# A two-layer trunk on one core: the FFN up-projections as 2x2 block products in seven multiplications

## The chip, the cores and the metric

The kernel runs on 1 core of one Trainium2 chip, in one launch. The metric is the device time in microseconds. Five engines matter: PE (TensorE, matmuls; PEld are its weight loads), DVE (VectorE), ACT (ScalarE), POOL (GpSimd) and SP (SyncE, which issues most DMAs). Tiles lie in SBUF; matmuls write to PSUM, which POOL doesn't read here.

## The reference, cut to what matters

Layer 0 is a retention block, layer 1 a differential attention; behind each stands the same kind of FFN, on 1024 positions of 1024 values, with D_FF = 2816. Only the FFN's up-projection changes:

```
def conv_ffn(xn, w_up, conv_w, conv_b, w_down):
    S = xn.shape[1]
    h = xn @ w_up                       # (1024 x 1024) @ (1024 x 5632)
    hp = jnp.pad(h, ((0, 0), (CONV_WIDTH - 1, 0), (0, 0)))
    hc = conv_b
    for j in range(CONV_WIDTH):         # causal, width 3, per channel
        hc = hc + hp[:, j:j + S] * conv_w[j]
    g, u = jnp.split(hc, 2, axis=-1)
    return (jax.nn.silu(g) * u) @ w_down

    x = x + rms_norm(h, a_norm_post[i])                  # end of the block before
    h = conv_ffn(rms_norm(x, ffn_norm_pre[layer]), ...)
    x = x + rms_norm(h, ffn_norm_post[layer])
```

## The kernel before

Every float32 operand of a matmul is kept as a high and a low part (`split_to`, L81: ACT rounds to the high part, DVE subtracts to get the low one), and a product is three matmuls: high x high, high x low, low x high (`mm3`, L96). Weights come through `load_w` (L85): a DMA on SP's queue into one of the two buffers of `raw`, POOL multiplies in the norm's gain where there is one, and ACT and DVE split into one of five `hl` buffers. PSUM has four tiles of 128 x 1024.

An FFN runs in `gated` (L479) over 22 blocks of 128 channels, in groups of 1, then nine times 2, then 3. For each block f, `up(f)` (L617) computes two column blocks of the up-projection, the gate's and the other (`proj_t`, 2 x 48 matmuls of 512 columns), the convolution out of PSUM (`conv`, L596: one ACT and two DVE instructions per column block), then silu on ACT, the product on POOL and the split of the result into one of three `act` buffers. `down` (L501) then multiplies a group's blocks by their rows of w_down for the 8 blocks of 128 positions, 12 matmuls each for a group of two, and DVE adds each PSUM result to `acc`. The down products of one group stand between the up-projections of the next. The last block is done in two halves (`up_last`, L652), whose second half stands between the first products of the last group.

`finish` (L129) is the end of a block: per 128 positions the norm, the residual, and for the next stage the transposes into `xt` (`into_xt`, L123); its last steps stand between the first up-projections. A scheduler places the instructions of every engine by their readiness and keeps program order only inside the stretches marked as manual; a buffer of a pool is reused when the last reader of its old tile is done, and DMAs stand in SP's queue in the order in which the scheduler put them. A wait at the head of an engine's queue holds everything behind it.

## Time and profile before

| | us |
|---|---|
| median of 3 runs | 2941.19 (2940.98 to 2942.84) |
| the profiled execution | 2942.96, its span 2941.2 |
| busy: PE, PEld | 2880.3, 2436.4 |
| busy: DVE, ACT, POOL | 1469.9, 946.5, 668.4 |
| granted TensorE clock, mean | 0.995 of full speed |

A share of busy time is a mean over stages: the first FFN lies between about 865 and 1608 us of the span, the second between about 2175 and the end. What a change inside a stage is worth is read from that stage's rows: how many matmuls, at which distance, and what ended the idle time before them. A granted clock of 1.00 is 2.4 GHz, 0.50 is 1.2 GHz.

### The profile page before, as it was taken

What the parts mean: (1) busy time and instruction counts of PE and PEld (TensorE: products, weight loads), DVE (VectorE), ACT (ScalarE), POOL (GpSimd) and SP (SyncE); (2) the same over time, 40 slices, a digit from 0 to 9 for tenths busy, and PEclk for the clock granted to TensorE, in tenths of its full rate; (3) what the DMA queues carried; (4) which work ended last, traced back from release to release, by engine and by line L of the source; (5) the groups of instructions that cost most, each with busy time, mean ns of one, the idle gap of its engine ahead of it and who ended that gap; (6) DMA issues with size and microseconds to landing.
All of it is one profiled execution on the core that took longest, in us unless ns stands there. A gap on an engine that the chain in (4) does not pass through costs nothing. (4 is left out here: it accounts for less than half of the span.)

```text
span 2941.2 us, 35261 instructions
## 1 busy us (share of the span) xinstructions
PE 2880.3 (98%) x14452; PEld 2436.4 (83%) x14452; DVE 1469.9 (50%) x1722; ACT 946.5 (32%) x1462; POOL 668.4 (23%) x744
## 2 busy tenths in 40 slices
PE   8999999999999999999999999999999999999998
PEld 7898989888877888888888788888777888888886
DVE  4433433434446444444445687777554444444445
ACT  3323222211134222222224565555453222222222
POOL 1111120000033111211114334444332121121113
PEclk9999999999999999999999999999999999999999
DMA  4111111321232111111113332233252111111112
GB/s 141 53 54 51 51 52 37 121 79 59 78 122 86 51 50 43 51 50 51 43 44 120 118 80 75 68 85 93 73 204 80 43 50 51 47 47 44 58 58 100
DMA packets 86225, 210.45 MB, mean 72 GB/s; under 512 B 9648, under 2 KB 35248, under 8 KB 86064
## 3 DMA queue, kind: packets, MB, share of 16 engines
q1 hardware_dynamic: 62432, 180.67, 19.3%
q10 hardware_dynamic: 23632, 27.53, 2.9%
q8 instruction: 114, 1.87, 0.3%
q14 instruction: 47, 0.39, 0.0%
HBM read 164.12 MB, written 31.46 MB: 66 GB/s over the span
## 5 line engine op out<-in xcount | busy, mean ns | idle before, releaser
L97 PE MATMUL ps<-xh,hl 128*128 128x512 f32 x1952 | 764.3, 392 | 3.7 <-DVE xl L83 2.4
L99 PE MATMUL ps<-xh,hl 128*128 128x512 f32 x1952 | 762.3, 391 | 0.0
L98 PE MATMUL ps<-xl,hl 128*128 128x512 f32 x1952 | 760.0, 389 | 0.5 <-DVE xl L83 0.5
L492 PE MATMUL ps<-hl,act 128*128 128x512 f32 x2880 | 664.5, 391 | 1.1 <-DVE acc L508 1.1
L492 PEld LDWEIGHTS ps<-hl,act 128*128 128x128 f32 x2880 | 540.8, 188 | 114.3 <-DVE acc L508 1.9
L604 DVE SCALAR_TENSOR_TENSOR hc<-ps,cw,hc 128x1023 f32<-128x1023 f32 (+4 forms) x184 | 226.6, 1232 | 536.8 <-ACT hc L600 536.5
L90 POOL TENSOR_TENSOR raw<-raw,gains 128x1024 f32<-128x1024 f32 x120 | 238.0, 1984 | 1124.3 <-DMA raw<-in_w_up 1032.7
L99 PEld LDWEIGHTS ps<-xh,hl 128*128 128x128 f32 x1952 | 366.9, 188 | 79.7
L97 PEld LDWEIGHTS ps<-xh,hl 128*128 128x128 f32 x1952 | 367.0, 188 | 79.6 <-DVE xl L83 2.6
L98 PEld LDWEIGHTS ps<-xl,hl 128*128 128x128 f32 x1952 | 366.8, 188 | 78.8 <-DVE xl L83 1.0
L82 ACT ACTIVATE hl<-raw 128x1024 fp32r<-128x1024 f32 x228 | 240.0, 1054 | 500.3 <-PE ps L492 320.0
L83 DVE TENSOR_TENSOR hl<-raw,hl 128x1024 fp32r<-128x1024 f32 x228 | 289.9, 1272 | 114.2 <-ACT hl L82 114.0
L510 DVE TENSOR_TENSOR acc<-ps,acc 128x1024 f32<-128x1024 f32 x192 | 234.6, 1222 | 148.4 <-PE ps L492 147.1
L600 ACT ACTIVATE hc<-ps,cw 128x1024 f32<-128x1024 f32 (+1 forms) x92 | 107.6, 1170 | 485.1 <-PE ps L99 475.7
L611 POOL TENSOR_TENSOR hc<-hc 128x1024 f32<-128x1024 f32 x42 | 100.8, 2400 | 346.8 <-DVE hc L604 319.9
L97 PE MATMUL ps<-hl,xh 128*128 128x256 f32 x544 | 154.9, 286 | 1.7 <-ACT xh L82 1.7
L99 PE MATMUL ps<-hl,xl 128*128 128x256 f32 x544 | 155.3, 286 | 0.8 <-DVE xl L83 0.7
L98 PE MATMUL ps<-hl,xh 128*128 128x256 f32 x544 | 154.8, 285 | 0.0
L853 ACT ACTIVATE s<-s,m 128x256 f32<-128x256 f32 (+7 forms) x128 | 99.1, 775 | 102.1 <-POOL m L852 101.7
L82 ACT ACTIVATE act<-hc 128x1024 fp32r<-128x1024 f32 (+1 forms) x46 | 47.1, 1024 | 239.9 <-POOL hc L611 231.1
L97 PEld LDWEIGHTS ps<-hl,xh 128*128 128x128 f32 x544 | 105.2, 194 | 2.8 <-ACT xh L82 2.6
L99 PEld LDWEIGHTS ps<-hl,xl 128*128 128x128 f32 x544 | 105.3, 194 | 1.6 <-DVE xl L83 1.5
(188 smaller groups left out, 3701.1 us busy)
## 6 DMA issues: line engine op xcount, KB each, us to landing
raw<-in_w_up SPq DMA_DIRECT2D x88, 512.0 KB, 3.5
raw<-in_w_down SPq DMA_DIRECT2D x44, 512.0 KB, 3.5
raw<-in_w_t SPq DMA_DIRECT2D x32, 512.0 KB, 3.5
xold<-x SPq DMA_DIRECT2D x24, 512.0 KB, 4.6
raw<-in_w_v SPq DMA_DIRECT2D x16, 512.0 KB, 3.5
oret<-t ACTq DMA_DIRECT2D x32, 256.0 KB, 2.3
raw<-in_a_w_out SPq DMA_DIRECT2D x16, 512.0 KB, 3.6
on<-oret SPq DMA_DIRECT2D x16, 512.0 KB, 4.6
```

The lines of the kernel that those rows point to most:

```text
L82: nc.scalar.activation(out=hi, in_=src, func=AF.Copy)
L83: nc.vector.tensor_tensor(out=lo, in0=src, in1=hi.bitcast(F32), op=ALU.subtract)
L90: nc.gpsimd.tensor_tensor(out=v, in0=v, in1=gain.unsqueeze(2).broadcast_to([P, gain.shape[1], n]), op=ALU.mult)
L97: nc.tensor.matmul(out, sh, mh, start=start, stop=False)
L98: nc.tensor.matmul(out, sh, ml, start=False, stop=False)
L99: nc.tensor.matmul(out, sl, mh, start=False, stop=stop)
L492: nc.tensor.matmul(ps[:, half, :], a, ws[f][:, m, hs], start=f == 0 and n == 0, stop=f == len(ws) - 1 and n == 2)
L510: nc.vector.tensor_tensor(out=acc[sb], in0=flat(ps), in1=acc[sb], op=ALU.add)
L600: nc.scalar.activation(out=hc[:, c0:c1], in_=ps[:, c0:c1], func=AF.Identity, scale=cw[0][:, n, 2:3], bias=cw[0][:, n, 3:4])
L604: nc.vector.scalar_tensor_tensor(out=hc[:, b:c1], in0=ps[:, b - j:c1 - j], scalar=cw[0][:, n, 2 - j:3 - j], in1=hc[:, b:c1], op0=ALU.mult, ...
L611: eng.tensor_tensor(out=hg[:, cs], in0=hg[:, cs], in1=hu[:, cs], op=ALU.mult)
L853: nc.scalar.activation(out=s[:, :w], in_=s[:, :w], func=AF.Exp, scale=0.125, bias=m, accum_out=l[:, c:c + 1])
```

## The change

The up-projection of a block f, [gate; other] = [A11 A12; A21 A22] x [X11 X12; X21 X22], is taken as a 2x2 block product: the rows are the two column blocks of w_up, the inner halves are k = 0 to 3 and 4 to 7, the columns are the two halves of 512 positions. Seven products of 4 x 3 matmuls (`prod`) take the place of eight, in Winograd's form: sums of A (s1 = A21 + A22, s2 = s1 - A11, A11 - A21, A12 - s2) are made by POOL in `weights(f)` and split into a ring of eight `wc` buffers; sums of X (t1, t2, t3, t4 and X22) are made once per layer by DVE and POOL and split. DVE adds the products' results while it takes them out of PSUM (`plus`), ACT copies out the first two. The products A11 X11 and A12 X21 of the first four f stand in the tail of the stage before and behind it. The norm's gain is now multiplied into the rows before the transposes (DVE, `finish`), no longer into the weights by POOL; `Staged` keeps the transposed rows of X unsplit as well.

The convolution reads SBUF tiles, not PSUM. Each finished block is stored to DRAM on ACT's queue, and only when all 22 are done a second phase runs `gated`, in which `up` is `stored`: load a block back through `raw`, split it into an `act` buffer. `up_last` is gone. Matmuls on a PSUM bank that already holds a product are added onto it (`onto`). In the second layer's output projection `load_o` takes its rows through `raw` too.

```diff
...
             nc.tensor.transpose(ps[:, k, :], xn[:, k * P:(k + 1) * P], ident)
         return ps
+    class Staged:
+        def __init__(self, pool, gain):
+            self.gain = gain
+            self.h, self.l = (pool.tile([P, NK, 512], F32R, name=f"x{n}0", tag=f"x{n}0") for n in "hl")
+            self.raw = [pool.tile([P, NK, 512], F32, name=f"xraw{c}", tag=("xh1", "xl1")[c]) for c in range(2)]
+            self.pool = pool
+        def put(self, ps, c, cols):
+            if c == 0:
+                split_to(self.h[:, :, cols], self.l[:, :, cols], ps)
+            nc.scalar.activation(out=self.raw[c][:, :, cols], in_=ps, func=AF.Copy)
     def into_xt(ps, sb, xt):
-        xh, xl = xt
         c, b = divmod(sb, 4)
         cols = slice(b * P, (b + 1) * P)
+        if isinstance(xt, Staged):
+            xt.put(ps, c, cols)
+            return
+        xh, xl = xt
         split_to(xh[c][:, :, cols], xl[c][:, :, cols], ps)
     def finish(mm, add, pool, psp, gpost, x_old, x_new, xt, order=tuple(range(NS)), turn_first=False, late=()):
...
                     xh = live["xh", c] = pool.tile([P, D], F32, name="xhn", tag="w4")
-                    nc.scalar.activation(out=xh, in_=live.pop(("t", c)), func=AF.Copy, scale=live.pop(("q", c)))
+                    if isinstance(xt, Staged):
+                        nc.vector.scalar_tensor_tensor(out=xh, in0=live.pop(("t", c)), scalar=live.pop(("q", c)),
+                                                       in1=xt.gain, op0=ALU.mult, op1=ALU.mult)
+                    else:
+                        nc.scalar.activation(out=xh, in_=live.pop(("t", c)), func=AF.Copy, scale=live.pop(("q", c)))
...
         return up
-    def ffn_up(wk, layer, xt, tail, w_pool=None, late=None, on_drained=None):
-        cw = []
-        gpre = gains4[:, 2 + layer, :]
...
+    def ffn_up(layer, xt, tail, w_pool, late, on_drained):
+        N_PRE = 4
+        acts = [dram.tile([P, S], F32, name=f"act{layer}_{f}") for f in range(NF)]
+        K0, K1 = slice(0, 4), slice(4, 8)
+        X11, X21 = ((xt.h[:, ks], xt.l[:, ks]) for ks in (K0, K1))
+        def prod(out, w, x, onto=False):
+            for k in range(4):
+                ws = slice(k * P, (k + 1) * P)
+                mm3(out, w[0][:, ws], w[1][:, ws], x[0][:, k, :], x[1][:, k, :], not onto and k == 0, k == 3, onto)
+        def load_halves(f, half):
+            raw = rawp.tile([P, 1024], F32, name="raw")
+            for u in range(2):
+                nc.sync.dma_start(out=raw[:, COLS[u]], in_=A["w_up"][layer, f + u][:, COLS[half]])
+            return raw
+        w_first = {}
+        def load_pre():
+            for f in range(0, N_PRE, 2):
+                hl = w_pool.tile([P, 2, 1024], F32R, name="hl", tag="hl")
+                split_to(hl[:, 0, :], hl[:, 1, :], load_halves(f, 0))
+                for u in range(2):
+                    w_first[f + u] = hl[:, 0, COLS[u]], hl[:, 1, COLS[u]]
+        if late is None:
+            load_pre()
+        else:
+            late.append(load_pre)
+        pre = []
+        for f in range(N_PRE):
+            if f % 2 == 0:
+                next(tail)
+                pre.append(psp.tile([P, 2, 512], F32, name="ps"))
+            prod(pre[-1][:, f % 2, :], w_first[f], X11)
+        for _ in tail:
+            pass
+        st = ExitStack()
+        on_drained()
+        up = st.enter_context(tc.tile_pool(name=f"u{layer}", bufs=7, reuse_waits="tile"))
+        sp = st.enter_context(tc.tile_pool(name=f"s{layer}", bufs=3, reuse_waits="tile"))
+        cp = st.enter_context(tc.tile_pool(name=f"c{layer}", bufs=1, reuse_waits="tile"))
+        ring = st.enter_context(tc.tile_pool(name=f"ring{layer}", bufs=8, reuse_waits="tile"))
+        gp = st.enter_context(tc.tile_pool(name=f"gu{layer}", bufs=1, reuse_waits="tile"))
+        cw = gp.tile([P, 2 * NF, 4], F32, name="cw")
+        nc.sync.dma_start(out=cw, in_=A["conv"][layer])
+        def half_tile():
+            return up.tile([P, 512], F32, name="u")
+        first = {}
+        def copied(f, bank):
+            first[f] = half_tile()
+            nc.scalar.activation(out=first[f], in_=bank, func=AF.Copy)
+        def split_part(src, eng=nc.vector):
+            t = ring.tile([P, 2, 512], F32R, name="wc")
+            nc.scalar.activation(out=t[:, 0, :], in_=src, func=AF.Copy)
+            eng.tensor_tensor(out=t[:, 1, :], in0=src, in1=t[:, 0, :].bitcast(F32), op=ALU.subtract)
+            return t[:, 0, :], t[:, 1, :]
+        for f in range(N_PRE):
+            if f % 2 == 0:
+                raw = load_halves(f, 1)
+            w = split_part(raw[:, COLS[f % 2]])
+            bank = pre[f // 2][:, f % 2, :]
+            copied(f, bank)
+            prod(bank, w, X21, True)
+        names = ("t2", "t3", "t1", "t4", "x22")
+        ops = {n: [cp.tile([P, 4, 512], F32R, name=n + u) for u in "hl"] for n in names}
+        r1, r2 = xt.raw
+        for b in range(4):
+            cols = slice(b * P, (b + 1) * P)
+            x11, x21, x12, x22 = r1[:, K0, cols], r1[:, K1, cols], r2[:, K0, cols], r2[:, K1, cols]
+            t2 = sp.tile([P, 4, P], F32, name="t2raw", tag="s")
+            def both(n, src, eng):
+                h, l = (t[:, :, cols] for t in ops[n])
+                nc.scalar.activation(out=h, in_=src, func=AF.Copy)
+                eng.tensor_tensor(out=l, in0=src, in1=h.bitcast(F32), op=ALU.subtract)
+            nc.vector.tensor_tensor(out=x11, in0=x12, in1=x11, op=ALU.subtract)
+            nc.vector.tensor_tensor(out=t2, in0=x22, in1=x11, op=ALU.subtract)
+            both("t2", t2, nc.vector)
+            nc.vector.tensor_tensor(out=x12, in0=x22, in1=x12, op=ALU.subtract)
+            both("t3", x12, nc.vector)
+            both("t1", x11, nc.gpsimd)
+            nc.gpsimd.tensor_tensor(out=x21, in0=x21, in1=t2, op=ALU.subtract)
+            both("t4", x21, nc.vector)
+            both("x22", x22, nc.gpsimd)
+        bufs = [xt.pool.tile([P, 4, S], F32, name=f"hbuf{c}", tag=("xh1", "xl1")[c]) for c in range(2)]
+        hb = [bufs[c][:, j, :] for j in range(4) for c in range(2)]
+        def h_tile():
+            return hb.pop(0)
+        h_first = {}
+        def take_first(f, bank):
+            h_first[f] = h_tile()
+            nc.scalar.activation(out=h_first[f][:, :512], in_=bank, func=AF.Copy)
+        def weights(f):
+            g, u = load_raw(A["w_up"][layer, f]), load_raw(A["w_up"][layer, NF + f])
+            a11, a12, a21, a22 = g[:, COLS[0]], g[:, COLS[1]], u[:, COLS[0]], u[:, COLS[1]]
+            if f >= N_PRE:
+                yield split_part(a11)
+            s1 = sp.tile([P, 512], F32, name="s1", tag="s")
+            s2 = sp.tile([P, 512], F32, name="s2", tag="s")
+            nc.gpsimd.tensor_tensor(out=s1, in0=a21, in1=a22, op=ALU.add)
+            nc.gpsimd.tensor_tensor(out=s2, in0=s1, in1=a11, op=ALU.subtract)
+            yield split_part(s2)
+            nc.gpsimd.tensor_tensor(out=a21, in0=a11, in1=a21, op=ALU.subtract)
+            yield split_part(a21)
+            yield split_part(s1)
+            if f >= N_PRE:
+                yield split_part(a12)
+            yield split_part(a22)
+            nc.gpsimd.tensor_tensor(out=a12, in0=a12, in1=s2, op=ALU.subtract)
+            yield split_part(a12)
+        def conv(n, src):
+            hc = h_tile()
+            nc.scalar.activation(out=hc, in_=src, func=AF.Identity, scale=cw[:, n, 2:3], bias=cw[:, n, 3:4])
+            for j in (1, 2):
+                nc.vector.scalar_tensor_tensor(out=hc[:, j:], in0=src[:, :S - j], scalar=cw[:, n, 2 - j:3 - j],
+                                               in1=hc[:, j:], op0=ALU.mult, op1=ALU.add)
+            return hc
+        def plus(out, bank, u):
+            nc.vector.tensor_tensor(out=out, in0=bank, in1=u, op=ALU.add)
+        ready = list(weights(0))
+        for f in range(NF):
+            ws = iter(ready)
+            coming, ready = (weights(f + 1) if f + 1 < NF else iter(())), []
+            def step():
+                got = next(coming, None)
+                if got is not None:
+                    ready.append(got)
+            full = f >= N_PRE
+            pq = psp.tile([P, 2, 512], F32, name="ps")
+            cd = psp.tile([P, 2, 512], F32, name="ps")
+            if full:
+                a, b = pq[:, 0, :], pq[:, 1, :]
+                prod(a, next(ws), X11)
+                copied(f, a)
+                step()
+            else:
+                b = pq[:, 0, :]
+                if f == 0:
+                    for i in range(N_PRE):
+                        take_first(i, pre[i // 2][:, i % 2, :])
+            c, d = cd[:, 0, :], cd[:, 1, :]
+            prod(b, next(ws), ops["t2"])
+            u2 = half_tile()
+            plus(u2, b, first.pop(f))
+            step()
+            prod(c, next(ws), ops["t3"])
+            u3 = half_tile()
+            plus(u3, c, u2)
+            step()
+            prod(d, next(ws), ops["t1"])
+            hu = h_tile()
+            plus(hu[:, 512:], d, u3)
+            step()
+            if full:
+                prod(a, next(ws), X21, True)
+                take_first(f, a)
+                step()
+            prod(c, next(ws), ops["t4"])
+            plus(hu[:, :512], c, u3)
+            step()
+            prod(d, next(ws), ops["x22"], True)
+            hg = h_first.pop(f)
+            plus(hg[:, 512:], d, u2)
+            ready.extend(coming)
+            cg = conv(f, hg)
+            hb.append(hg)
+            cu = conv(NF + f, hu)
+            hb.append(hu)
+            nc.scalar.activation(out=cg, in_=cg, func=AF.Silu)
+            nc.gpsimd.tensor_tensor(out=cg, in0=cg, in1=cu, op=ALU.mult)
+            nc.scalar.dma_start(out=acts[f], in_=cg)
+            hb.extend((cg, cu))
+        st.close()
+        return acts
+    def stored(wk, acts):
+        def up(i):
+            raw = load_raw(acts[i])
+            act = wk.actp.tile([P, 2, S], F32R, name="act")
+            split_to(act[:, 0, :], act[:, 1, :], raw)
+            return act
+        return up
+    COLS = (slice(0, 512), slice(512, 1024))
...
     gpost = load_gain(wk.gp, "gpost", A["a_norm_post"])
-    nxt = new_xt(xtp)
+    nxt = Staged(xtp, load_gain(wk.gp, "gpre", A["ffn_pre_rows"][0]))
...
         return finish(mm, add, wk.w4, psp, g, x1, x2, xt3[0])
-    tail = gated(wk, ffn_up(wk, 0, xt, tail), NF, rows(A["w_down"][0], NF), last)
+    def drained():
+        wk.mid.close()
+        wk.ops.close()
+    acts = ffn_up(0, xt, tail, wk.hlp, None, drained)
+    open_ops(wk, "f")
+    open_mid(wk, "f", "left")
+    tail = gated(wk, stored(wk, acts), NF, rows(A["w_down"][0], NF), last)
...
     gpost = load_gain(g5, "gpost", A["b_norm_post"])
-    xt = new_xt(xtb)
+    xt = Staged(xtb, load_gain(g5, "gpre", A["ffn_pre_rows"][1]))
     heads_t = {}
     sums = {}
     def load_o(sb):
         e0 = DH - 1 if sb < N_BESIDE else 0
-        if e0 == 0:
-            on = o5.tile([P, D], F32, name="on", bufs=2)
-        else:
-            on = rawp.tile([P, 1024], F32, name="raw")
+        on = rawp.tile([P, 1024], F32, name="raw")
...
         p5.close()
-        open_ops(wk, "b")
-        open_mid(wk, "b", "right")
     def last(mm, add):
         g = load_gain(wk.gp, "gpost", A["ffn_norm_post"][1])
         return finish(mm, add, wk.w4, psp, g, x3, x_out, None)
-    tail = gated(wk, ffn_up(wk, 1, xt, tail, o5, late, drained), NF, rows(A["w_down"][1], NF), last)
+    acts = ffn_up(1, xt, tail, o5, late, drained)
+    open_ops(wk, "b")
+    open_mid(wk, "b", "right")
+    tail = gated(wk, stored(wk, acts), NF, rows(A["w_down"][1], NF), last)
```

Left out of the diff: `mm3` passes `onto` to its three matmuls, `gains4` shrinks to two rows, the code for `up_last` in `gated` goes, and the gain's layout in DRAM is now by rows.

On SP, in the first FFN between two groups' down products, two loads of w_down (`raw<-in_w_down`) were followed by four of the next blocks' up weights. Before:

```order
L78 DMA raw_7572<-in_w_up 128x1024
L78 DMA raw_7630<-in_w_up 128x1024
L78 DMA raw_7693<-in_w_down 128x1024
L78 DMA raw_7698<-in_w_down 128x1024
L78 DMA raw_7817<-in_w_up 128x1024
L78 DMA raw_7875<-in_w_up 128x1024
L78 DMA raw_7940<-in_w_up 128x1024
L78 DMA raw_7998<-in_w_up 128x1024
```

Now, at the same place in the down phase (act0_4 is the stored block of f = 4, the second of its group; act0_5 the first of the next group; the two w_down rows are those of the group of f = 3 and 4):

```order
L78 DMA raw_10110<-act0_4_6341 128x1024
L78 DMA raw_10115<-act0_5_6342 128x1024
L78 DMA raw_10120<-in_w_down 128x1024
L78 DMA raw_10125<-in_w_down 128x1024
L78 DMA raw_10242<-act0_6_6343 128x1024
L78 DMA raw_10247<-act0_7_6344 128x1024
L78 DMA raw_10252<-in_w_down 128x1024
```

The two loads of stored blocks now stand ahead of the two of w_down, in the same two buffers.

On PE, the end of a group's down products was followed by an up-projection whose weights (hl_9292) are another load's. Before:

```order
L492 MATMUL ps_9273<-hl_9167,act_8792 128x512 x6
L492 MATMUL ps_9273<-hl_9172,act_9037 128x512 x6
L97 MATMUL ps_9295<-xh0_4373,hl_9292 128x512
L98 MATMUL ps_9295<-xl0_4375,hl_9292 128x512
L99 MATMUL ps_9295<-xh0_4373,hl_9292 128x512
```

Now the next group follows; hl_10122 and hl_10127 are split from raw_10120 and raw_10125 above, act_9898 is the buffer into which raw_10110 is split as act_10112:

```order
L513 MATMUL ps_10096<-hl_9990,act_9898 128x512 x6
L513 MATMUL ps_10096<-hl_9995,act_9980 128x512 x6
L513 MATMUL ps_10130<-hl_10122,act_9985 128x512 x2
L513 MATMUL ps_10144<-hl_10122,act_9985 128x512 x2
L513 MATMUL ps_10158<-hl_10122,act_9985 128x512 x2
L513 MATMUL ps_10172<-hl_10122,act_9985 128x512 x2
L513 MATMUL ps_10130<-hl_10122,act_9985 128x512 x4
L513 MATMUL ps_10144<-hl_10122,act_9985 128x512 x4
L513 MATMUL ps_10158<-hl_10122,act_9985 128x512 x4
L513 MATMUL ps_10172<-hl_10122,act_9985 128x512 x3
L513 MATMUL ps_10130<-hl_10127,act_10112 128x512 x2
```

No other matmul stands between the groups, and the new group's first ones go over four PSUM tiles.

On POOL, at the start of the first FFN, the sums of X and the first weight sums now stand in this row (L703 and L696 are of X, L726 makes s1, L727 s2); before, POOL had one multiplication by the gain per weight load there:

```order
L703 TENSOR_TENSOR xraw0_4375<-xraw0_4375,t2raw_6974 128x4x128
L696 TENSOR_TENSOR t1l_6939<-xraw0_4375,t1h_6938 128x4x128
L696 TENSOR_TENSOR x22l_6943<-xraw1_4376,x22h_6942 128x4x128
L703 TENSOR_TENSOR xraw0_4375<-xraw0_4375,t2raw_6989 128x4x128
L696 TENSOR_TENSOR t1l_6939<-xraw0_4375,t1h_6938 128x4x128
L726 TENSOR_TENSOR s1_7010<-raw_7008 128x512
L696 TENSOR_TENSOR x22l_6943<-xraw1_4376,x22h_6942 128x4x128
L696 TENSOR_TENSOR t1l_6939<-xraw0_4375,t1h_6938 128x4x128
L696 TENSOR_TENSOR x22l_6943<-xraw1_4376,x22h_6942 128x4x128
L727 TENSOR_TENSOR s2_7011<-s1_7010,raw_7006 128x512
```

From the first row of t1l to s2_7011 they are nine.

## Rows read from the trace of the kernel before

**Rows 1.** The page: busy us, share, instructions; then the clock in 40 slices.

```profile
PE 2880.3 (98%) x14452; PEld 2436.4 (83%) x14452; DVE 1469.9 (50%) x1722; ACT 946.5 (32%) x1462; POOL 668.4 (23%) x744
...
PEclk9999999999999999999999999999999999999999
```

**Rows 2.** Stages: from:to, length, busy us and instructions by engine, clock, DMA.

```profile
863.70:870.40 6.70, 5.55 (x17) 4.75 (x18) 3.55 (x3) 4.32 (x7) 6.09 (x6) 0.50 0.43 158
...
904.70:908.00 3.30, 3.01 (x14) 3.02 (x15) 0.21 (x1) 2.29 (x3) 2.00 (x2) 0.50 0.33 135
960.00:1600.00 640.00, 640.00 (x2825) 530.17 (x2824) 290.35 (x240) 152.73 (x148) 126.91 (x66) 1.00 0.17 52
```

**Rows 3.** Groups by line and shape, 960 to 1600 us: busy, mean ns, idle before.

```profile
L492 PE MATMUL ps<-hl,act 128*128 128x512 f32 x930 | 212.7, 389 | 0.0
...
L83 DVE TENSOR_TENSOR hl<-raw,hl 128x1024 fp32r<-128x1024 f32 x58 | 70.6, 1217 | 11.1 <-ACT hl L82 11.1
L82 ACT ACTIVATE hl<-raw 128x1024 fp32r<-128x1024 f32 x58 | 61.1, 1053 | 102.7 <-PE ps L492 99.7 <-POOL rstd L104 3.0
L604 DVE SCALAR_TENSOR_TENSOR hc<-ps,cw,hc 128x1023 f32<-128x1023 f32 x38 | 48.7, 1283 | 242.1 <-ACT hc L600 242.1
...
L83 DVE TENSOR_TENSOR act<-hc,act 128x512 fp32r<-128x512 f32 x1 | 0.7, 691 | 0.7 <-ACT act L82 0.7
L82 ACT ACTIVATE act<-hc 128x512 fp32r<-128x512 f32 x1 | 0.6, 632 | 2.3 <-DVE hc L611 2.3
```

**Rows 4.** TensorE's waits, whole span: us in total, times, longest.

```profile
PE ps L120 <- ACT xhn L186: 13.6, 9, 3.7
```

**Rows 5.** In order of time, 1030 us: start, length, instruction, idle before.

```profile
1030.01 0.39 PE L99 MATMUL ps<-xh,hl 128*128 128x512 f32 x1
...
1030.43 1.21 ACT L600 ACTIVATE hc<-ps,cw 128x1024 f32<-128x1024 f32 x1 [9.81 <-PE ps L99]
```

**Rows 6.** In order of time, 1021 to 1027 us: DVE, SP's queue, POOL.

```profile
1021.57 1.21 DVE L83 TENSOR_TENSOR hl<-raw,hl 128x1024 fp32r<-128x1024 f32 x1
...
1022.81 0.33 SPq L78 DMA_DIRECT2D raw<-in_w_up  x1
1026.31 1.90 POOL L90 TENSOR_TENSOR raw<-raw,gains 128x1024 f32<-128x1024 f32 x1 [20.00 <-DMA raw<-in_w_up]
```

**Rows 7.** TensorE in order of time, around the first FFN's start.

```profile
864.85 1.97 PE L120 MATMUL ps<-ident,xhn 128*128 128x128 f32 x8 [3.70 <-ACT xhn L186]
866.47 6.25 PE L492 MATMUL ps<-hl,act 128*128 128x512 f32 x18
872.56 1.03 PE L120 MATMUL ps<-ident,xhn 128*128 128x128 f32 x8
...
877.55 1.03 PE L120 MATMUL ps<-ident,xhn 128*128 128x128 f32 x8
...
904.99 3.44 PE L120 MATMUL ps<-ident,xhn 128*128 128x128 f32 x16 [2.85 <-ACT xhn L186]
909.54 0.72 PE L97 MATMUL ps<-xh,hl 128*128 128x512 f32 x2 [1.11 <-ACT xh L82]
```

**Rows 8.** Groups by line and shape, whole span, of POOL, DVE and ACT.

```profile
L611 POOL TENSOR_TENSOR hc<-hc 128x1024 f32<-128x1024 f32 x42 | 100.8, 2400 | 346.8 <-DVE hc L604 319.9 <-ACT hc L610 15.8 <-issue 11.2
...
L346 POOL TENSOR_TENSOR t<-t,t 128x512 f32<-128x512 f32 x32 | 46.3, 1456 | 155.7 <-DVE t L345 151.8 <-issue 3.9
...
L83 DVE TENSOR_TENSOR atl<-pst,ath 128x512 fp32r<-128x512 f32 x48 | 32.6, 682 | 2.3 <-ACT ath L82 2.2
...
L82 ACT ACTIVATE xh<-ps 128x1024 fp32r<-128x1024 f32 x32 | 32.4, 1018 | 16.4 <-PE ps L120 15.9
```

**Rows 9.** The page: DMA queues, packets, MB, share of 16 engines.

```profile
q1 hardware_dynamic: 62432, 180.67, 19.3%
```

**Rows 10.** In order of time, 1048 to 1052 us: POOL and DVE.

```profile
1048.66 1.90 POOL L90 TENSOR_TENSOR raw<-raw,gains 128x1024 f32<-128x1024 f32 x1
...
1049.83 1.81 DVE L83 TENSOR_TENSOR act<-hc,act 128x1024 fp32r<-128x1024 f32 x1 [3.67 <-ACT act L82]
```

More of the change, by code (lines that the diff above doesn't have):

```diff
@@ L94, in load_w, with mm3 @@
         return hl
-    def mm3(out, sh, sl, mh, ml, start, stop):
-        nc.tensor.matmul(out, sh, mh, start=start, stop=False)
-        nc.tensor.matmul(out, sh, ml, start=False, stop=False)
-        nc.tensor.matmul(out, sl, mh, start=False, stop=stop)
+    def mm3(out, sh, sl, mh, ml, start, stop, onto=False):
+        nc.tensor.matmul(out, sh, mh, start=start, stop=False, skip_group_check=onto)
+        nc.tensor.matmul(out, sh, ml, start=False, stop=False, skip_group_check=onto)
+        nc.tensor.matmul(out, sl, mh, start=False, stop=stop, skip_group_check=onto)
     def rstd(ss, eps):
@@ L325, in trunk @@
                     v_split(v0, 0, c, ps)
-            for i in range(2):
-                nc.sync.dma_start(out=gains4[:, 2 + i, :], in_=A["ffn_norm_pre"][i])
             nc.sync.dma_start(out=gains4[:, 0, :], in_=A["b_norm_pre"])
@@ L589, in ret_up @@
         return up
-    def ffn_up(wk, layer, xt, tail, w_pool=None, late=None, on_drained=None):
-        cw = []
-        gpre = gains4[:, 2 + layer, :]
-        def conv(n, ps, hc, c0, c1):
-            if not cw:
-                cw.append(wk.gp.tile([P, 2 * NF, 4], F32, name="cw"))
-                nc.sync.dma_start(out=cw[0], in_=A["conv"][layer])
-            nc.scalar.activation(out=hc[:, c0:c1], in_=ps[:, c0:c1], func=AF.Identity, scale=cw[0][:, n, 2:3],
-                                 bias=cw[0][:, n, 3:4])
-            for j in (1, 2):
-                b = max(c0, j)
-                nc.vector.scalar_tensor_tensor(out=hc[:, b:c1], in0=ps[:, b - j:c1 - j],
-                                               scalar=cw[0][:, n, 2 - j:3 - j],
-                                               in1=hc[:, b:c1], op0=ALU.mult, op1=ALU.add)
-        def gate(hg, hu, act, c0, c1, eng):
-            cs = slice(c0, c1)
-            nc.scalar.activation(out=hg[:, cs], in_=hg[:, cs], func=AF.Silu)
-            eng.tensor_tensor(out=hg[:, cs], in0=hg[:, cs], in1=hu[:, cs], op=ALU.mult)
-            split_to(act[:, 0, cs], act[:, 1, cs], hg[:, cs])
-        def tiles():
-            return [wk.w4.tile([P, S], F32, name="hc", tag="w4") for _ in range(2)]
-        def up(f):
-            ns = (f, NF + f)
-            if f == NF - 1:
-                return up_last(ns)
-            pss = []
-            if f == 0:
-                ws = []
-                def load():
-                    ws.extend(load_w(w_pool or wk.hlp, A["w_up"][layer, n], gpre) for n in ns)
-                if late is None:
-                    load()
-                else:
-                    late.append(load)
-                for u in range(2):
-                    next(tail)
-                    pss.append(psp.tile([P, S], F32, name="ps"))
-                    proj_t(pss[u], ws[u], xt, (0,))
-                for _ in tail:
-                    pass
-                for ps, w in zip(pss, ws):
-                    proj_t(ps, w, xt, (1,))
-                if on_drained is not None:
-                    on_drained()
-            hc = tiles()
-            for u, n in enumerate(ns):
-                if f > 0:
-                    w = load_w(wk.hlp, A["w_up"][layer, n], gpre)
-                    pss.append(psp.tile([P, S], F32, name="ps"))
-                    proj_t(pss[u], w, xt)
-                conv(n, pss[u], hc[u], 0, S)
```

30 lines of the change are left out of this document (2 added, 28 removed).

## The prediction

> **What bounds the kernel now.** I read the share of busy time first: TensorE is busy 98% of the span, no other engine above 50%, and the clock row shows its full 2.4 GHz in nearly every slice [rows 1]. Then the table by stage: in a stretch inside the first FFN TensorE issues 2825 matmuls in 640.00 us, all 640 busy at a granted clock of 1.00, one per 0.2265 us [rows 2]. The groups by line of that stretch say that the others keep up: matmuls show almost no idle time before them, while DVE, ACT and POOL wait for each other [rows 3]. The waits of TensorE over the whole span are small: the largest kind, of the transposes at the ends of stages, comes to 13.6 us in 9 times [rows 4]. So a matmul of 512 columns taken away is worth 0.2265 us, as long as nothing new makes TensorE wait.
>
> **Part 1, the products.** Before, one f is 2 column blocks x 2 halves x 8 k x 3 = 96 matmuls of 512 columns; now it is 7 products x 4 k x 3 = 84. Over 22 f and 2 layers that is 528 fewer: 528 x 0.2265 = 119.6 us off the path. This saving is certain, and every other part is a cost.
>
> **Part 2, group boundaries of the down phase.** Before, a group's weights w_down were loaded and split while TensorE did the up-projection of the next f's (two column blocks of 48 matmuls stand for each f), so nothing waited. Now down groups follow each other directly, and SP's order matters: between two pairs of w_down stand two loads of stored blocks, all through the two buffers of `raw`. The first stored block of the pair (raw_10110) is split into one of three `act` buffers, and that buffer is read by the running group up to its last row block: 7 matmuls before the group ends (6 on the second block follow it). The next pair member holds the other `raw` buffer in the same way. So the next group's w_down isn't even requested until the running group ends, and behind it are all of the next group's matmuls. The chain, from the start of the last matmul that reads the buffer: matmul 0.39 and ACT 0.03 later [rows 5], ACT half of the split 1.05 [rows 3], DVE half 1.21, SP's issue 0.03, 3.50 from the issue to the reader's start [rows 6], ACT half of w_down 1.05, and two hand-overs of 0.04: 7.34 us. TensorE has 7 x 0.2265 = 1.59 us of work meanwhile, so it stands for 5.75 us. Its order agrees: the new group starts with two matmuls on each of four PSUM tiles, those that need only the first half of the weights. The second weights come about 4 us after the first and find 24 matmuls (5.4 us) ahead of them, so I count no second wait.
>
> The clock adds to it. After an idle of 3.70 us the granted clock was 0.50, so 1.2 GHz, and 18 matmuls with 8 transposes took 7.71 us (864.85 to 872.56), against 4.99 for the next 26 of the same kind (872.56 to 877.55), at full clock: 2.7 us lost. It fell after 2.85 us of idle too, where 16 transposes took 3.44 us against about 1.6 (8 take 0.79) [rows 2, 7]: some 1.7 lost. A wait of 5.75 us is longer than either, so I take 2.0 at each. The 22 blocks make 11 groups; the first two find buffers free, the other nine have this wait: 18 in both layers x 7.75 = 139.5 us. Bounds: 18 x 5.75 = 103.5 if the clock stays up, 18 x 8.45 = 152 with the larger loss.
>
> **Part 3, from up to down.** The first w_down load waits for a `raw` buffer whose DVE split stands behind the last sum of the up phase. From TensorE's last matmul: 0.2 to the sum, 0.68 for it (the 512-column PSUM row of [rows 8]), 1.21, 0.03, 3.50, 1.05: 6.7 us. But SP first issues a gain and four `xold` loads of 512 KB, freed by that same matmul. Queue q1 moved 180.67 MB in 19.3% of 2941 us, 1.65 us for 512 KB [rows 9]; five of them ahead make 8.2 us, and the load lands at about 12, ready at 13. Between 6.7 and 13 I take 10, and 2 for the clock: 24 us for both layers, bounds 13 and 30.
>
> **Part 4, from the tail to up.** Now TensorE has 36 matmuls (8.2 us) of the pre-products after the last transposes, then needs the sums t2 and the first weight sum s2. POOL makes s2 as the last of 9 instructions from t1's low half on (its order), at 1.456 each [rows 8] 13.1 us, starting when ACT has copied the last rows (1.02), split four weights and three operands (7 x 0.63): at 5.4. With ACT's half of the split, 19.2. TensorE is done with its cover at 1.02 + 0.63 + 8.15 = 9.8: 9.4 us idle, 2 for the clock, less the 1.11 that stood there before [rows 7]: 10 a layer, 20 in all. Bounds: 4 a layer if POOL's operations took half of that row, 20 if DVE's 13 splits of about 0.69 there have to go between them.
>
> **Part 5, the up phase itself.** TensorE works 84 x 0.2265 = 19.03 us for a full f, 60 x 0.2265 = 13.59 for the first four. DVE gets 7 splits (5 in the first four) of 512 columns at 0.69 [rows 3], 5 sums out of PSUM at 0.68, 4 convolution steps at 1.28: 13.35 (11.97). POOL gets 4 sums at 1.456 and the gate at 2.40: 8.22 [rows 8]. Alone each fits. But a DVE operation with both inputs in SBUF doesn't run beside POOL: one began at 1049.83 while POOL was busy until 1050.56, and ended at 1051.64, 1.08 after POOL [rows 10], where 1.22 is the usual whole. If POOL's time falls only on DVE's PSUM sums and idle time, the pair needs 9.95 + 8.22 = 18.2 us (16.8 in the first four) and TensorE sets the pace of the phase: 4 x 16.8 + 18 x 18.2 is 394 us, its own 397. If it never does, 21.57 (20.2): 469 us, 72 more. I take a third, 24 a layer, 48 in all, since the scheduler lets TensorE work some ten microseconds ahead of the sums; bounds 0 and 144.
> The Trainium skill ("SBUF — State Buffer", section "SBUF: two separate sides") calls the pair of ports that DVE shares with GpSimd an exclusive lock, held for the whole instruction. The row at 1049.83 agrees. By it the upper bound is the likelier end; it is the second rival below.
>
> The remaining edits are taken at nothing: the stores of finished blocks on ACT's queue and their loads (2 x 44 x 0.52 = 46 MB) meet DMA engines that q1 fills to 19.3% [rows 9], and each block is read back many groups after its store; the changed tail scales its rows on DVE and not on ACT, one instruction for one in the chain of part 4; `load_o` of layer 1 shares `raw` with the first weight loads, and if that cover fails it costs one load, 3.5 us.
>
> **Sum.** -119.6 + 139.5 + 24 + 20 + 48 = +111.9. The profiled execution took 2942.96 us (span 2941.2), so 3054.9; the median of the runs is 1.8 lower: **3053 us**.
>
> **Rivals.** (a) Faster: a group's weights come early after all, because a `raw` buffer is free during the running group; then only parts 3 to 5 are paid, 2941 - 119.6 + 92 = 2914, and with no cost in part 5, 2866. It decides below (119.6 - 92)/18 = 1.5 us per boundary. Loads are well hidden in the kernel before; against it, the order has both buffers taken at each of the 18 places. (b) The up phase goes at the pace of DVE and POOL one after the other: +72 a layer and not 24, 3053 + 96 = 3149. For it, the row of the DVE split that ended 1.08 after POOL; against it, sums out of PSUM can run beside POOL. (c) The clock stays up at the boundaries: 3053 - 18 x 2 = 3017. Against it, both idles of 2.85 and 3.70. (d) The second weights of a group are late too, since they pass the same buffers one DVE split later: some 3 us more at 18 places, 3107. (e) That the products aren't fewer is excluded by the counts of part 1.
>
> **Chances.** Forecast 0.50, (b) 0.18, (c) 0.14, (d) 0.11, (a) 0.07. The measurement can tell about 0.2% (6 us) from no change. Only (a) gives a faster kernel, 0.06 of its 0.07; 0.02 within 0.2%; slower 0.92. Range: all lower bounds together give 2941 - 119.6 + 103.5 + 13 + 8 = 2946, all upper ones 2941 - 119.6 + 152 + 30 + 40 + 144 = 3187; it would take several ends at once, so 2968 to 3150.
>
> **What would show it.** Part 1: 528 fewer matmuls, and stretches at 0.2265 us each. Part 2: in the down phase eighteen idles of TensorE of about 5.8 us at distances of some 29 us, released by ACT's split of w_down, each with a stretch of half clock. Part 3 and 4: one idle of 7 to 13 and one of 4 to 17 us in each layer. Part 5: DVE splits stretched wherever POOL runs, and TensorE waiting for DVE in the first f's. The forecast is wrong if w_down lands while the running group still multiplies, or if idle time inside the up phase exceeds that of the boundaries.

## The result, and the profile after

The changed kernel takes 3116.6 us (median of 4 runs, 3113.7 to 3120.8) against 2941.6 for the kernel before on the same chip: a ratio of 1.0595, 95% interval 1.0577 to 1.0614. It is slower by 175 us, where 112 were forecast.

The page of the changed kernel's profile (part 1 and the clock row of part 2), which answers to [rows 1]:

```profile
span 3116.0 us, 35617 instructions
...
PE 2849.9 (91%) x13924; PEld 2382.0 (76%) x13924; DVE 1856.3 (60%) x2200; ACT 1094.4 (35%) x1790; POOL 834.8 (27%) x858
...
PEclk9999999999988999999988999999998999999888
```

TensorE issues 528 matmuls fewer, as counted, and stands idle 205 us more (3116.0 less 2849.9, against 2941.2 less 2880.3). It is busy only 30 us less, not 119.6, since matmuls at the low clock count as busy for longer. The table of its waits says where (engine, group, releaser: us in total, times, longest), to be held against [rows 4]:

```profile
PE ps L513 <- ACT hl L82: 125.8, 20, 13.0
PE ps L98 <- ACT wc L672: 20.5, 14, 5.9
PE ps L121 <- DVE xhn L206: 18.3, 6, 6.1
PE ps L121 <- ACT xhn L209: 13.8, 3, 11.9
PE ps L98 <- DVE hbuf L747: 12.7, 13, 1.7
PE ps L100 <- DVE wc L673: 8.5, 5, 3.7
...
PE ps L98 <- ACT u L668: 7.3, 2, 5.5
...
PE ps L121 <- ACT xraw L137: 4.3, 2, 3.0
```

The first row is the 18 boundaries and the two switches from the up to the down phase. Cut by stages (busy us and instructions of PE, PEld, DVE, ACT, POOL, then the granted clock, DMA share and GB/s), layer 0 first: tail, start up to the first product with t2, up phase, switch, down phase to the first transposes; then the same of layer 1, its down phase to the end. Of the 48 matmuls with X21 that belong to the first four f, 36 stand in the start; the last 12 stand behind the first products with t2, so the up phase has 1764:

```profile
869.47:924.69 55.22, 42.18 (x184) 34.08 (x185) 44.07 (x33) 25.12 (x37) 33.61 (x33) 0.84 0.24 95
924.69:945.84 21.15, 13.18 (x36) 9.43 (x36) 21.15 (x19) 13.49 (x26) 16.00 (x11) 0.71 0.14 50
945.84:1383.15 437.31, 413.57 (x1763) 330.34 (x1764) 319.21 (x342) 180.03 (x252) 193.29 (x109) 0.99 0.22 79
1383.15:1395.57 12.42, 0.39 (x2) 0.00 (x1) 6.58 (x7) 3.83 (x4) 2.34 (x1) 0.67 0.80 303
1395.57:1707.97 312.40, 249.35 (x984) 200.82 (x984) 155.91 (x129) 51.03 (x52) 16.05 (x12) 0.89 0.23 79
2271.45:2332.72 61.27, 48.47 (x237) 39.17 (x235) 45.02 (x40) 36.21 (x55) 23.22 (x30) 0.92 0.37 130
2332.72:2352.50 19.78, 14.19 (x37) 10.23 (x38) 11.33 (x16) 8.78 (x17) 14.57 (x9) 0.56 0.15 53
2352.50:2772.09 419.59, 410.17 (x1765) 331.92 (x1763) 319.84 (x341) 178.92 (x249) 184.21 (x105) 0.99 0.23 82
2772.09:2785.47 13.38, 0.38 (x2) 0.00 (x0) 6.56 (x7) 3.96 (x4) 2.34 (x1) 0.67 0.98 392
2785.47:3116.00 330.53, 265.01 (x1056) 214.16 (x1056) 173.19 (x143) 52.87 (x59) 26.59 (x22) 0.89 0.23 80
```

Read the clock column beside the length: the up phases keep 0.99 and lose time all the same, the down phases fall to 0.89. (The counts of a stretch can be off by one at its edges.)

One boundary of layer 0, in order of time (start, us, engine, line, what it writes from what, idle before and its releaser):

```profile
1430.60 1.06 ACT L82 ACTIVATE act<-raw 128x1024 fp32r<-128x1024 f32 x1 [19.33 <-PE ps L513]
1431.70 1.23 DVE L83 TENSOR_TENSOR act<-raw,act 128x1024 fp32r<-128x1024 f32 x1 [1.23 <-ACT act L82]
...
1432.95 2.60 SPq L78 DMA_DIRECT2D raw<-in_w_down  x2
...
1436.36 1.06 ACT L82 ACTIVATE hl<-raw 128x1024 fp32r<-128x1024 f32 x1 [3.34 <-DMA raw<-in_w_down]
...
1437.47 2.93 PE L513 MATMUL ps<-hl,act 128*128 128x512 f32 x6 [5.54 <-ACT hl L82]
```

This is the forecast's chain link by link: the stored block could be split only when the running group stopped reading `act`; its DVE half freed `raw`; only then was w_down requested, 3.4 us later it was there, and TensorE stood for 5.54 us. Behind each of the 18 idles, which are 5.50 to 5.79 us long, the granted clock is 0.50. Here are the first matmuls behind this one, then a longer stretch:

```profile
1437.47:1440.31 2.84, 2.84 (x7) 2.29 (x8) 1.67 (x2) 1.06 (x1) 0.00 (x0) 0.50 0.40 130
...
1437.47:1678.14 240.67, 195.62 (x768) 157.66 (x768) 115.11 (x97) 33.85 (x32) 0.00 (x0) 0.90 0.21 70
```

The second row holds eight groups and eight boundaries: 30.08 us each, of which 96 x 0.2265 = 21.74 is work; 8.34 lost, some 5.6 idle and 2.7 by the clock.

### The profile page after: what moved, and what is told of

Its sections match the earlier page's. It is cut to its first block, busy times and chain, and to the rows that moved or that the text cites. A ratio compares the mean times of both kernels' runs of the same rounds, so it can differ in the third digit from the quotient of the medians.

```text
span 3116.0 us, 35617 instructions
## 1 busy us (share of the span) xinstructions
PE 2849.9 (91%) x13924; PEld 2382.0 (76%) x13924; DVE 1856.3 (60%) x2200; ACT 1094.4 (35%) x1790; POOL 834.8 (27%) x858
## 5 line engine op out<-in xcount | busy, mean ns | idle before, releaser
L513 PE MATMUL ps<-hl,act 128*128 128x512 f32 x2880 | 714.5, 412 | 126.9 <-ACT hl L82 125.8
L83 DVE TENSOR_TENSOR hl<-raw,hl 128x1024 fp32r<-128x1024 f32 x144 | 184.7, 1283 | 173.8 <-ACT hl L82 173.6
L673 DVE TENSOR_TENSOR wc<-raw,wc 128x512 fp32r<-128x512 f32 x212 | 183.2, 873 | 92.3 <-ACT wc L672 90.7
L98 PE MATMUL ps<-xh,hl 128*128 128x512 f32 x576 | 225.5, 391 | 2.6 <-DVE xl L83 2.4
L99 PE MATMUL ps<-xl,hl 128*128 128x512 f32 x576 | 224.5, 390 | 0.3 <-DVE xl L83 0.3
L100 PE MATMUL ps<-xh,hl 128*128 128x512 f32 x576 | 224.4, 390 | 0.0
L742 DVE SCALAR_TENSOR_TENSOR hbuf<-hbuf,cw,hbuf 128x1023 f32<-128x1023 f32 (+1 forms) x132 | 199.0, 1508 | 40.2 <-ACT hbuf L740 38.7
L672 ACT ACTIVATE wc<-raw 128x512 fp32r<-128x512 f32 x212 | 132.1, 626 | 180.1 <-DMA raw<-in_w_up 65.8
L90 POOL TENSOR_TENSOR raw<-raw,gains 128x1024 f32<-128x1024 f32 x32 | 67.7, 2116 | 340.8 <-DVE hl L83 292.0
L98 PE MATMUL ps<-xh,wc 128*128 128x512 f32 x320 | 131.1, 412 | 23.0 <-ACT wc L672 12.1
L740 ACT ACTIVATE hbuf<-hbuf,cw 128x1024 f32<-128x1024 f32 x88 | 109.2, 1240 | 104.8 <-DVE hbuf L747 93.5
L100 PE MATMUL ps<-xh,wc 128*128 128x512 f32 x320 | 130.4, 408 | 5.8 <-DVE wc L673 5.8
L99 PE MATMUL ps<-xl,wc 128*128 128x512 f32 x320 | 129.5, 405 | 0.0
```

The source lines that it names most:

```text
L83: nc.vector.tensor_tensor(out=lo, in0=src, in1=hi.bitcast(F32), op=ALU.subtract)
L98: nc.tensor.matmul(out, sh, mh, start=start, stop=False, skip_group_check=onto)
L99: nc.tensor.matmul(out, sh, ml, start=False, stop=False, skip_group_check=onto)
L100: nc.tensor.matmul(out, sl, mh, start=False, stop=stop, skip_group_check=onto)
L513: nc.tensor.matmul(ps[:, half, :], a, ws[f][:, m, hs], start=f == 0 and n == 0, stop=f == len(ws) - 1 and n == 2)
L672: nc.scalar.activation(out=t[:, 0, :], in_=src, func=AF.Copy)
```

## Experiments

Times are medians; the changed kernel is 3116.6, the kernel before 2940 to 2942 in every comparison.

**1. w_down a group earlier.** The forecast's largest term by itself (`early` is set in both FFNs):

```diff
...
-        def down(first, acts, ids):
-            ws = [load_w(wk.hlp, w_down[i]) for i in ids]
+        def weights_of(ids):
+            return [load_w(wk.hlp, w_down[i]) for i in ids]
+
+        def down(first, acts, ids, ws):
+            ws = ws or weights_of(ids)
...
             acts = []
+            ws = weights_of(ids) if early else None
             for u, i in enumerate(ids):
                 acts.append(up(i))
                 if u == 0 and todo is not None:
                     down(*todo)
-            todo = (gi == 0, acts, ids)
+            todo = (gi == 0, acts, ids, ws)
...
```

> The changed kernel, but in the down phase a group's w_down is loaded ahead of the same group's stored blocks, a whole group earlier; the same instructions and buffers otherwise. Theory (a group's weights are requested only when the running group ends): the 18 idles of about 5.6 us and their half-clock stretches go, 18 x 8.3 = 150 us, and the first w_down of each layer no longer stands behind a gain and four xold loads, up to 2 x 8: 2950 to 2970 us. Rival (the second stored block of a group, whose buffer comes free only with the running group's last matmul, takes the place of the weights): 2 to 4 us idle stay at each boundary, 3030 to 3060. Rival (the boundaries are slow for a reason other than the order of the loads): within 10 us of 3117.

Measured: 2959.6 us, 157 less; ratio to before 1.0065 (1.0051 to 1.0079). The rows are the two down phases, which were 312.40 and 330.53, and the wait for the weights, which was 125.8 us in 20 times:

```profile
1389.87:1629.22 239.35, 226.23 (x985) 185.19 (x985) 156.70 (x132) 52.62 (x54) 16.90 (x13) 0.98 0.35 116
2699.78:2961.40 261.62, 243.15 (x1056) 200.34 (x1056) 173.10 (x146) 54.36 (x61) 27.51 (x23) 0.97 0.34 115
```
```profile
PE ps L513 <- ACT hl L82: 7.4, 2, 3.7
```

142 us leave the down phases (7.9 per boundary), 17.6 the two switches (25.8 us together before, 8.2 now), and the clock is back at 0.97 to 0.98. So the order of the loads made the waits; the blocks' buffer didn't take the weights' place.

**2. POOL's work in the up phase on DVE** (sums of the weights, splits of t1 and x22, the sum t4, the gate's product):

```diff
-            both("t1", x11, nc.gpsimd)
+            both("t1", x11, nc.vector)
...
-            nc.gpsimd.tensor_tensor(out=s1, in0=a21, in1=a22, op=ALU.add)
+            nc.vector.tensor_tensor(out=s1, in0=a21, in1=a22, op=ALU.add)
...
-            nc.gpsimd.tensor_tensor(out=cg, in0=cg, in1=cu, op=ALU.mult)
+            nc.vector.tensor_tensor(out=cg, in0=cg, in1=cu, op=ALU.mult)
```

> The changed kernel, but everything that POOL does in the up phase (sums of the weights, two of the splits of X, the sum t4, the gate's product) is done by DVE. Theory (DVE and POOL take turns when a DVE operation has both inputs in SBUF, so POOL's work costs DVE more than it saves): DVE's own work for a full f is 13.35 + 4 x 0.69 + 1.22 = 17.3 us, under TensorE's 19.03; the up phase loses its idle (44 us in both layers against the products' own time) and the start of it shortens by 5 to 15 us a layer: 3045 to 3065 us. Rival (DVE and POOL work beside each other and DVE is short of time): DVE gets 3.98 us more per f, the up phase becomes slower by 0 to 50 us: 3117 to 3170.

Measured: 3061.8 us, 55 less; ratio 1.0413 (1.0398 to 1.0427). The up phases take 403.95 and 407.17 us in place of 437.31 and 419.59, at 4 more microseconds of DVE work per f. Groups by line and form from 980 to 1340 us, first the changed kernel, then this one (mean ns of one; idle before):

```profile
L673 DVE TENSOR_TENSOR wc<-raw,wc 128x512 fp32r<-128x512 f32 x87 | 74.7, 866 | 51.0 <-ACT wc L672 49.7
L742 DVE SCALAR_TENSOR_TENSOR hbuf<-hbuf,cw,hbuf 128x1023 f32<-128x1023 f32 x27 | 42.6, 1578 | 17.0 <-ACT hbuf L740 16.9
L673 DVE TENSOR_TENSOR wc<-s,wc 128x512 fp32r<-128x512 f32 x36 | 40.1, 1114 | 12.3 <-ACT wc L672 12.3
L747 DVE TENSOR_TENSOR hbuf<-ps,u 128x512 f32<-128x512 f32 x55 | 37.4, 682 | 1.6 <-PE ps L100 1.6
...
L729 POOL TENSOR_TENSOR raw<-raw 128x512 f32<-128x512 f32 x18 | 36.0, 2001 | 0.0
```
```profile
L673 DVE TENSOR_TENSOR wc<-raw,wc 128x512 fp32r<-128x512 f32 x92 | 62.4, 685 | 4.9 <-ACT wc L672 4.7
L747 DVE TENSOR_TENSOR hbuf<-ps,u 128x512 f32<-128x512 f32 x59 | 40.5, 686 | 24.5 <-PE ps L100 23.1 <-DMA act<-hbuf 1.3
L742 DVE SCALAR_TENSOR_TENSOR hbuf<-hbuf,cw,hbuf 128x1023 f32<-128x1023 f32 x30 | 38.4, 1279 | 6.2 <-ACT hbuf L740 5.9
...
L673 DVE TENSOR_TENSOR wc<-s,wc 128x512 fp32r<-128x512 f32 x37 | 25.3, 683 | 0.5 <-ACT wc L672 0.5
...
L729 DVE TENSOR_TENSOR raw<-raw 128x512 f32<-128x512 f32 x18 | 12.3, 683 | 0.0
```

What reads SBUF twice is stretched beside POOL (0.87 and 1.11 us for 0.68); the sum out of PSUM isn't (0.682 and 0.686). A weight sum that took POOL 2.0 us takes DVE 0.68. But DVE wasn't short of time on the whole: over the first layer's up phase it is busy for longer without POOL, 340.69 us in place of 319.21 (by the sums of their lengths its own instructions lose 54 us of stretch, and 83 us of POOL's former work come to it):

```profile
943.20:1347.15 403.95, 400.58 (x1765) 330.50 (x1763) 340.69 (x446) 180.29 (x249) 0.00 (x0) 1.00 0.26 85
```

So POOL did save DVE time, and the theory's reason, that it costs DVE more than it saves, is wrong. What went is DVE's idle time in front of the splits, waiting for ACT's half (49.7 and 12.3 us in the first rows, 4.7 and 0.5 in the second): the sums on POOL, and the weights' loads, came later there. The edit takes away the stretch and these later sums together, so how much of the 55 us each made isn't shown.

**3. The residual of the first FFN's tail on DVE:**

```diff
-                    residual(a, nc.vector if turn_first or t == NS or t == NS - 1 and xt is None else nc.gpsimd)
+                    residual(a, nc.vector if turn_first or isinstance(xt, Staged) or t == NS or t == NS - 1 and xt is None else nc.gpsimd)
```

> The changed kernel, but in the tail ahead of the first FFN the residual's sum is on DVE and not on POOL (in the second layer's tail it is there already). Theory (the row scaling that moved from ACT to DVE waits for POOL's residual sum, 3.4 us in place of 1.3, and makes the transposes late): the scaling falls to about 1.3 us, the waits of transposes for it in that tail from 16.7 to under 9 us, and the kernel gains 6 to 12 us: 3105 to 3111. Rival (the chain is long because DVE has one more instruction per row block, and gets another): the same or up to 8 us slower, 3115 to 3125.

Measured: 3107.9 us, 8.7 less (ratio 1.0570, 1.0555 to 1.0584). In the changed kernel the scaling of a row block lies over POOL's sum:

```profile
871.98 2.37 POOL L174 TENSOR_TENSOR acc<-acc,xold 128x1024 f32<-128x1024 f32 x1
872.04 3.38 DVE L206 SCALAR_TENSOR_TENSOR xhn<-acc,rstd,gpre 128x1024 f32<-128x1024 f32 x1 [0.72 <-POOL rstd L105]
```

It ends 1.07 us after POOL. The eight of the tail, in the changed kernel and in this one:

```profile
L206 DVE SCALAR_TENSOR_TENSOR xhn<-acc,rstd,gpre 128x1024 f32<-128x1024 f32 x8 | 21.4, 2678 | 4.3 <-POOL rstd L105 4.3
```
```profile
L206 DVE SCALAR_TENSOR_TENSOR xhn<-acc,rstd,gpre 128x1024 f32<-128x1024 f32 x8 | 11.2, 1405 | 5.1 <-POOL rstd L105 5.1
```

The tail falls from 55.22 to 48.57 us, with seven residual sums more on DVE. TensorE's waits for these rows in that tail fall from 16.7 to 11.5 us, where under 9 were expected.

**4. The next stage's gain on DVE.** At the end of the first layer TensorE waits 11.9 us (`ps L121 <- ACT xhn L209`), where the longest such wait was 1.5 before (between 1580 and 1660 us of its span):

```profile
PE ps L120 <- ACT xhn L186: 4.4, 5, 1.5
```

```diff
-            nc.gpsimd.tensor_tensor(out=v, in0=v, in1=gain.unsqueeze(2).broadcast_to([P, gain.shape[1], n]),
+            nc.vector.tensor_tensor(out=v, in0=v, in1=gain.unsqueeze(2).broadcast_to([P, gain.shape[1], n]),
```

> The changed kernel, but the gain is multiplied into the weights of the second layer's projections by DVE and not by POOL; around the end of the first FFN POOL does four of these ahead of the norm's chain. Theory (at the end of the first down phase TensorE waits 11.9 us for the transposes because POOL's gain products stand in the chain): the wait falls to under 6 us, 6 to 12 us are gained: 3105 to 3111. Rival (the wait is there because the last group no longer has half of an up-projection beside it to fill the chain's own length): the wait stays over 9 us, 3113 to 3119.

Measured: 3119.0 us (ratio 1.0604, 1.0589 to 1.0618): nothing gained. Waits between 1680 and 1765 us, in the changed kernel and in this one:

```profile
PE ps L121 <- ACT xhn L209: 13.8, 3, 11.9
PE ps L98 <- DVE xl L83: 2.4, 1, 2.4
```
```profile
PE ps L121 <- ACT xhn L209: 8.9, 3, 7.1
PE ps L98 <- DVE xl L83: 4.8, 1, 4.8
```

POOL's products did stand in the chain for 4.8 us, but half of that came back at the next stage's first products; where the rest went isn't shown. By the time the rival is right, by the wait neither.

**5. The transposes one row block later:**

```diff
-            d = at(t - 3)
+            d = at(t - 3 if t >= NS or turn_first else t - 4)
...
-                if t != NS - 1:
-                    turned = transposed(psp, live.pop(("xh", d))), d
+                turned = transposed(psp, live.pop(("xh", d))), d
```

> The changed kernel with the later transposes alone. Theory (the missing filler at the end of the first layer, 12 us, was no part of the forecast's sum): 5 to 12 us faster, 3105 to 3112, the wait of 11.9 us falls to about 7. Rival: the wait moves to the next transposes, 3114 to 3120.

Measured: 3107.3 us, 9.3 less (ratio 1.0567, 1.0552 to 1.0583), in the expected range for another reason. The wait of 11.9 us fell to 7.1, but this came back:

```profile
PE ps L121 <- ACT xhn L209: 9.1, 2, 7.1
PE ps L98 <- DVE xl L83: 8.6, 1, 8.6
```

From the down phase's start to the next tail it takes 6.7 us longer (882.6 against 875.9). The gain lies at the other place that the edit touches: the first FFN's tail, counted from its first transposes, shrank from 55.22 to 46.13 us (17 of its matmuls now stand ahead of them, in time that was idle), and the start and the up phase behind it by 6.1 together; why these two did isn't shown. The missing 12 us at the end of the first layer were shown in the trace; no edit got them back, and whether the lost half of an up-projection is their whole cause stays open.

**6. The copies of the pre-products first:**

```diff
+        for f in range(N_PRE):
+            copied(f, pre[f // 2][:, f % 2, :])
         for f in range(N_PRE):
...
-            bank = pre[f // 2][:, f % 2, :]
-            copied(f, bank)
-            prod(bank, w, X21, True)
+            prod(pre[f // 2][:, f % 2, :], w, X21, True)
```

> The changed kernel with the copies ahead alone. Theory of the forecast (the start ends with POOL's chain to the weight sum s2, whichever wait of TensorE comes before it): 0 to 5 us gained, 3112 to 3117, the wait shows before the first product with t2. Rival (the copies are what the start waits for): 10 to 20 us gained, 3097 to 3107.

Measured: 3097.8 us, 18.8 less (ratio 1.0532, 1.0518 to 1.0547). The time is the rival's, the place the forecast's: the wait of 5.5 us for the copy went, and that before the first product with t2 grew from 2.1 to 6.9, so the first layer's start takes 21.13 us as before (21.15). The chain to s2 does end it there. The start and the up phase:

```profile
924.14:945.27 21.13, 13.81 (x48) 10.41 (x49) 21.13 (x19) 12.55 (x24) 15.96 (x11) 0.82 0.16 51
945.27:1369.40 424.13, 407.94 (x1752) 329.87 (x1752) 322.52 (x342) 178.86 (x251) 188.74 (x109) 0.99 0.24 82
```

The start now holds all 48 matmuls, and the up phase takes 424.13 in place of 437.31 us: 2.7 of that are the 12 matmuls that moved, 10.5 are gained inside the phase. Why isn't shown. In the second layer the two stages together gain nothing (441 us for 440).

**7. Together.** First the edits of 1, 2 and 3:

> The three edits that paid, together: w_down a group earlier, the up phase's POOL work on DVE, the residual of the first FFN's tail on DVE. Theory (they lie one behind the other in time, at different places): the gains of the single runs add, 3116.6 - 157 - 55 - 8.7 = 2896 us, under the kernel before. Rival (with POOL's work on it, DVE is the next to be late, and part of the gain is lost): 2910 to 2945.

Measured: 2903.3 us, ratio 0.9873 (0.9858 to 0.9888): 1.3% under the kernel before. Of the 220.5 us that the three saved alone, 213.3 are there, so they nearly add; the time lies between the two expectations. With the later transposes of 5:

> The kernel with those three edits, and the transposes of a norm's tail stand one row block later in the program (behind the fifth row block's products and not the fourth's) in both tails of the first layer. Theory (in the last group nothing is left that fills the norm's chain, so TensorE waits about 10 us for the first transposes): a row block of 18 matmuls, 4.1 us, goes in front, and the half clock behind the wait gets shorter: 8 to 15 us faster than the kernel with three edits. Rival (the wait comes back at the next transposes): within 4 us of it.

Measured: 2901.8 us (ratio 0.9865, 0.9849 to 0.9882), 1.5 less: the rival. With the copies of 6 in place of that:

> The kernel with three edits, and ACT's copies of the four pre-product banks stand ahead of the first product that is added onto a bank. Theory (the wait of 6.5 to 7.0 us at the start of each up phase is the copy of the second bank: it shares a PSUM tile with the bank onto which the product before it is added, so it waits for that product and then stands behind 18 splits of X in ACT's queue): both waits go, with half of the 10 and 13.7 us at half clock, 12 to 22 us gained: 2881 to 2891. Rival (POOL's former chain, now DVE's, to the weight sum s2 ends as late, so the wait moves to the first product with t2): 2895 to 2904.

Measured: 2897.5 us, ratio 0.9850 (0.9837 to 0.9864), 5.9 less: the rival. In the first layer the wait of 7.0 us became one of 6.8 before the first product with t2; the gain is small because the start has its own chain. This is the fastest kernel of the study, 43 us under the kernel before:

```profile
span 2895.7 us, 35474 instructions
...
PE 2782.7 (96%) x13924; PEld 2351.0 (81%) x13924; DVE 1890.8 (65%) x2451; ACT 1094.6 (38%) x1790; POOL 388.4 (13%) x607
```

Its largest waits of TensorE are now those at the starts of the up phases and at the end of the first layer:

```profile
PE ps L98 <- ACT wc L676: 17.9, 4, 8.0
PE ps L121 <- ACT xhn L209: 12.8, 4, 9.6
```

## Why the prediction was right in its direction and 63 us short

The range held the time, and the bottleneck was named: the loads' order at the group boundaries. No cost came out smaller than forecast, so no error hid another. Each measured term is the length of a stretch less its matmuls at 0.2265 us.

| term | forecast | measured |
|---|---|---|
| products | -119.6 | 528 fewer: -119.6 |
| 18 boundaries | +139.5 | 18 x 8.34 = +150; taken away they gave 142 |
| switches | +24 | 12.0 + 13.0 idle, 2.8 each by the clock: +31 |
| starts | +20 | 21.15 + 19.78 less 36 matmuls (8.15) each, and 5.9 idle before the second: +31 |
| up phases | +48 | 437.31 + 419.59 less 1764 matmuls (399.5) each: +58 |
| tails | 0 | about +21 |
| end of layer 0 | 0 | 11.9 for 1.5 idle: +10 |

The sum is +181, 69 over the forecast's 112 and 6 more than the difference; the kernel before had small losses of its own in these stretches (1.11 us of idle ahead of its first up-projection, [rows 7]).

- **Part 1** held.
- **Part 2** held link by link: 5.5 to 5.8 idle, forecast 5.75. The clock's share was the short one, 2.7 and not 2.0; the row that gave its upper bound [rows 7] had 2.7 too. Rival (c) falls, since the clock was at 0.50 behind every boundary. Rival (d), whose 3107 us came nearest of all, came near by luck: no second wait stands behind the first. Rival (a) falls with the waits themselves, and experiment 1 shows that the order of the loads makes them.
- **Part 3**: the cause held. At the switch SP issued the gain and four xold loads, then at 1386.13 w_down, whose split began at 1394.46; DMA share 0.80 and 0.98 there. I had bounded its idle by 6.7 and 13 us and taken 10; it was 12 and 13, near the upper bound, which had all five loads moved ahead of it.
- **Part 4** was short, 31 for 20, within its bounds, and its mechanism held in the first layer only: there the chain to s2 ends the start (experiment 6), behind a wait of 5.5 us for ACT's copy that the forecast didn't see. In the second layer TensorE didn't wait for s2 at all. It stood 5.9 and 3.7 us for the splits of the pre-products' own weights and 1.9 for ACT's copy, none of which the forecast's chain held.
- **Part 5**: the size held, 58 us for 48, between its bounds and well under rival (b)'s 144. That POOL's work is the cause is shown by experiment 2, which leaves 12 of the 58. The stretch was there as foretold, and TensorE waited for DVE's sums (`hbuf L747`, 13 times) and late splits (`wc`). But the forecast priced a shortage of DVE's time, and DVE was busy 319 of 437 us and stood idle for late splits; how much is the stretch and how much POOL's later sums stays open.
- **"The remaining edits are taken at nothing"** is the step that failed. "One instruction for one" overlooked that the scaling of the rows went from ACT (1.13 to 1.15 us in that tail before, whether POOL ran beside it or not) to DVE, which doesn't run beside POOL: the rule of part 5, not applied to the tail. The first tail became 10.5 us longer (44.69 before, 55.22 after) and began 4.6 later; experiment 3 gives back 7.3 of these 15 us, and the rest isn't accounted for. The second tail became about 6 us longer (49.37 before; 61.27 less the 5.9 counted above), and there the scaling isn't stretched (1.41 us). The wait that is new in it, 4.3 us, is for ACT's copies of the transposed rows (`xraw L137`), one instruction more for each of the first four row blocks, which the forecast left out as well; no run tests it. The other omission is the end of layer 0: `up_last` had been named as filler of the last group, but its removal got no price.

Of these 69 us over the forecast's sum, 31 are the two terms that weren't in it, 11 the starts, 10 the up phases, 10 the boundaries and 7 the switches.

## What to carry to other kernels

When a fused loop is cut into two phases, draw the second phase's load order against its buffers: here loads whose target came free only when the running group ended stood, in the same queue and the same two buffers, ahead of the weights that TensorE needed first, and moving the weights ahead was worth 157 us, more than the 119.6 that the arithmetic saved. Where an operation changes its engine, ask not only how long it takes there but what that engine can't run beside. Giving work to a second engine saves the first one's time only as far as the two really overlap, and its slower instructions can still come late for a third engine: here the first engine was spared time, and taking the work back was worth 55 us all the same.
